# Eight of 22 pairs by Strassen's rule in the down projections of a two-layer encoder

## The chip, the cores and the metric

The kernel runs on one core of one Trainium2 chip. Its time is the device time of that core in microseconds. Five engines run their own queues side by side and wait for each other by semaphores: PE (TensorE, matmuls), DVE (VectorE), ACT (ScalarE), POOL (GpSimd, not used here but for set-up) and SP (SyncE, which issues the loads).

## The reference

A trunk of two layers over 256 tokens of width 2048, in float32. Each layer has a token mixer and a channel mixer, and each of the four does x = x + RMSNorm(f(RMSNorm(x))). What is changed lies in the channel mixer:

```python
D_MODEL, SEQ, D_FF, CONV_WIDTH = 2048, 256, 5632, 3

def conv_glu(h, w_up, conv_w, conv_b, w_down):
    u = h @ w_up
    gate, val = u[..., :D_FF], u[..., D_FF:]
    gate = depthwise_conv3(gate, conv_w, conv_b)
    return (jax.nn.gelu(gate, approximate=False) * val) @ w_down

for i in range(DEPTH):
    ...
    h = rms_norm(x, p['ffn_pre'])
    x = x + rms_norm(conv_glu(h, *p['ffn']), p['ffn_post'])
```

The down projection is the last product: (256 x 5632) by (5632 x 2048).

## The kernel before

**Numbers.** A float32 matrix is held as two parts for the matmuls, a rounded one and the rest: `whi` and `wlo` for weights, `gh` and `gl` for the activations of the channel mixer. A product is three matmuls (L1101, L1102, L1104): hi by hi, lo by hi, hi by lo. The weights arrive whole. `_split` (L159) makes the parts: ACT casts to `whi` (L173) and DVE subtracts it from the raw weights into `wlo` (L174). There are three buffers each for `whi` and `wlo`, and four for the raw weights, all used in turn.

**Chunks.** All weights are cut into chunks of 128 x 1024 floats (512 KB) in one list for the whole program. `weights` (L187) is called once for each chunk: it emits the splits of the chunks up to two further on and the loads (L148) up to five further on. A raw load waits only until its buffer has been split, so SP runs ahead of the other engines.

**Up projection.** `ffn` (L968) works through 11 groups of 512 channels. In each, `proj_t` makes gate and value, the convolution, Gelu and product follow on DVE and ACT, and four tiles of `gh` and `gl` come out. Work that is to lie between the matmuls is written as generators: `now` takes one on, and `tick` runs each up to its next `yield`, once for each chunk.

**Down projection.** `down` (L1002) makes 1024 columns of the output at a time (a half, h = 0 and 1), as two column groups of 512. The 5632 rows are 22 pairs of 256. A plain pair needs two chunks, one for each column group, with 2 token blocks x 2 row blocks x 3 matmuls each: 24 matmuls of 512 columns. `PAIRS` (6) of the pairs go by Strassen's rule in Winograd's form instead. There a pair is a 2 x 2 block product (token blocks, row blocks, column groups), and seven block products do for eight: 21 matmuls. For that, sums of weights (`Seven.sums`, four subtractions on DVE, L76) and sums of tokens (`sums` in `down`, L1010) are needed; the products are added up at the end (`added`, L1045). A seven pair has four steps:

- step 0: the products with the two weight blocks as they are; behind its split the sums of weights are made
- step 1: two products with sums of weights (in place of the blocks of step 0)
- step 2: two products with the second load, its first block by now a sum
- step 3: one product with `seven_t`, 512 columns

The two loads of a pair go to tiles `seven_a` and `seven_b`, one buffer each. The sums of tokens for two pairs at a time (one tile of `gh` and `gl`) take one add of 1024, four of 256, a cast and a subtraction; all three of them run at the start of the down projection.

**Order.** `down_order` (L38) mixes the steps with plain ones: `LEAD` plain steps ahead, then for each pair 0, plain, plain, 1, plain, 2, 3, plain, then the rest of the plain steps. A scheduler under the language sets the final order on each engine, within the dependencies.

Of the kernel before, what the change touches and what calls it, by code (L numbers as in the profile page):

```python
# [30 lines left out]

PAIRS = 6
LEAD = 5, 1


def down_order(h):  # L38

    plain = [("plain", p, o) for o in range(2) for p in range(PAIRS, KF // 2)]  # L40
    out, plain = plain[:LEAD[h]], deque(plain[LEAD[h]:])
    for p in range(PAIRS):
        for j in (0, None, None, 1, None, 2, 3, None):
            out.append(plain.popleft() if j is None else ("seven", p, j))
    return out + list(plain)


class Seven:
# [3 lines left out]


    def __init__(self, a, b):
        self.srcs, self.raw = (a, b), None

    def load(self, model):
        if self.raw is None:
            self.raw = []
            for src, tag in zip(self.srcs, "ab"):  # L60
                raw = model.room.tile([P, 1024], F32, tag=f"seven_{tag}", name=f"seven_{tag}", bufs=1)
                model.nc.sync.dma_start(out=raw, in_=src)
                self.raw.append(raw)

    def step(self, model, j):

        a, b = self.raw
        return (a, a, b, self.t2)[j] if j else a

    def sums(self, model):  # L70
        nc = model.nc
        a, b = self.raw
        self.t2 = model.room.tile([P, 512], F32, tag="seven_t", name="seven_t", bufs=1)
        a0, a1, b0, b1 = a[:, :512], a[:, 512:], b[:, :512], b[:, 512:]
        for out, x, y in ((a0, b0, a0), (self.t2, b1, a0), (a1, a1, self.t2), (b0, b1, b0)):
            nc.vector.tensor_tensor(out=out, in0=x, in1=y, op=ALU.subtract)  # L76

# [9 lines left out]
class Model:  # L87
# [60 lines left out]
    def _load(self, i):  # L148
        if i >= len(self.chunks) or i in self.loaded or i < self.at or i in self.made:
            return  # L150
        if isinstance(self.chunks[i], tuple):
            self.chunks[i][0].load(self)
            self.loaded[i] = None
            return
        raw = self.wp.tile([P, 1024], F32, tag="raw", name="raw", bufs=4)
        self.nc.sync.dma_start(out=raw, in_=self.chunks[i])
        self.loaded[i] = raw
# [810 lines left out]
    def ffn(self, layer, pre):  # L968
        nc, tc = self.nc, self.tc
        with tc.tile_pool(name=f"ffn{layer}", bufs=1) as sp:  # L970
            self.room = sp
            xs = self.xhl
            x = lambda k: xs[k // 4][:, k % 4].rearrange("p a t -> p (a t)")
            gh = [sp.tile([P, 4, T], F32R, name=f"gh{i}") for i in range(NFG)]
            gl = [sp.tile([P, 4, T], F32R, name=f"gl{i}") for i in range(NFG)]
            cw = lambda j, c: self.gain(f"l{layer}_conv_w", j * KF + c)
            norm = self.now(self.pre_norm(sp))
            for gi in range(NFG):
                pg = self.proj_t(KD, x, "acc")
                self.finish(norm)  # L980
                act = []
                for i in range(4):
                    c = 4 * gi + i
                    g = self.joined(sp, sp.tile([P, T], F32, tag="g", name="g", bufs=2), pg[i])
                    y = sp.tile([P, T], F32, tag="yf", name="yf", bufs=4)
                    nc.vector.tensor_tensor(out=g, in0=g, in1=self.rb, op=ALU.mult)
                    nc.scalar.activation(y, g, AF.Identity, scale=cw(1, c), bias=self.gain(f"l{layer}_conv_b", c))
                    nc.vector.scalar_tensor_tensor(out=y[:, 1:], in0=g[:, :T - 1], scalar=cw(0, c), in1=y[:, 1:],
                                                   op0=ALU.mult, op1=ALU.add)
                    nc.vector.scalar_tensor_tensor(out=y[:, :T - 1], in0=g[:, 1:], scalar=cw(2, c),  # L990
                                                   in1=y[:, :T - 1], op0=ALU.mult, op1=ALU.add)
                    nc.scalar.activation(y, y, AF.Gelu)
                    act.append(y)
                pv = self.proj_t(KD, x, "at")
                for i in range(4):
                    u = self.joined(sp, sp.tile([P, T], F32, tag="u", name="u", bufs=2), pv[i])
                    nc.vector.tensor_tensor(out=u, in0=u, in1=self.rb, op=ALU.mult)
                    nc.vector.tensor_tensor(out=u, in0=u, in1=act[i], op=ALU.mult)
                    self.parted(gh[gi][:, i, :], gl[gi][:, i, :], u)
            self.down(gh, gl, 2 * layer + 1, pre)  # L1000

    def down(self, gh, gl, post, pre):  # L1002

        nc = self.nc
        add = lambda out, a, b, op=ALU.add: nc.vector.tensor_tensor(out=out, in0=a, in1=b, op=op)  # L1005
        mm = nc.tensor.matmul
        ss = self.small.tile([P, 2, 4], F32, tag="ss", name="ss", bufs=2)
        seven, m, gains = [], [], []

        def sums():  # L1010

            for i in range(PAIRS // 2):
                tmp = self.act.tile([P, 2, 1024], F32, tag="xm3", name="sums")
                add(tmp[:, 0], gh[i].rearrange("p k t -> p (k t)").bitcast(F32),
                    gl[i].rearrange("p k t -> p (k t)").bitcast(F32))
                a = tmp[:, 0].rearrange("p (q k t f) -> p q k t f", q=2, k=2, t=2)
                s = tmp[:, 1].rearrange("p (q n f) -> p q n f", q=2, n=4)
                a11, a12, a21, a22 = (a[:, :, k, t] for t in range(2) for k in range(2))
                add(s[:, :, 0], a21, a22)
                add(s[:, :, 1], s[:, :, 0], a11, ALU.subtract)  # L1020
                add(s[:, :, 2], a11, a21, ALU.subtract)
                add(s[:, :, 3], a12, s[:, :, 1], ALU.subtract)
                yield
                seven.append(self.act.tile([P, 2, 4, 2, P], F32R, tag=f"xm{i}", name=f"seven{i}"))
                self.parted(seven[i][:, :, :, 0, :], seven[i][:, :, :, 1, :], s)
                yield

        def tokens(k, t):
            return tuple(g[k // 4][:, k % 4, t * P:(t + 1) * P] for g in (gh, gl))

        def summed(p, n):
            return tuple(seven[p // 2][:, p % 2, n, i, :] for i in range(2))

        def operands(kind, p, j, t):

            if kind == "plain":
                return [(2 * j + t, lambda k=2 * p + i: tokens(k, t), i) for i in range(2)]
            if t:
# [117 lines left out]
    def all_chunks(self):  # L1156
# [26 lines left out]
def _tiled(w, n=512):  # L1183

    k, m = w.shape
    b = 1024 // n
    w = w.reshape(k // (b * P), b, P, m // n, n).transpose(3, 0, 2, 1, 4)
    return np.ascontiguousarray(w).reshape(m // n, k // (b * P), P, 1024)


def _rope(pos, dim):

    inv = np.float32(10000.0) ** (-np.arange(0, dim, 2, dtype=np.float32) / np.float32(dim))
    ang = pos.astype(np.float32)[:, None] * inv.astype(np.float32)[None, :]
    c, s = np.cos(ang).astype(np.float32), np.sin(ang).astype(np.float32)
    return np.stack([np.concatenate([c, c], axis=1), np.concatenate([-s, s], axis=1)], axis=1)
# [50 lines left out]
```

## Time and profile before

| | |
|---|---|
| median of three runs | 2062.05 us (2062.04 to 2070.98) |
| span of the profiled execution, first to last instruction | 2060.1 us |
| PE busy in the span | 2043.4 us |
| DVE busy in the span | 1478.4 us |
| ACT busy in the span | 1129.3 us |
| loads and stores | 384 MB, 186 GB/s over the span |
| up projection, layer 0 | about 331 to 823 us |
| down projection, layer 0 | about 823 to 1051 us |
| down projection, layer 1 | about 1818 to 2047 us |

How to read the rows: a row of the timeline has start, duration, engine, line, operation, output<-input, shape and, in brackets, how long the engine had been idle and who released it. A row of a stretch has its bounds and length, then the busy time of PE, its weight loads, DVE, ACT and POOL with the instructions started, PE's granted clock, DMA's busy share and GB/s. A row of loads has the tile, the count, the size and the microseconds from issue to landing. SP's rows show when a load is issued, not how long it takes. Matmuls are pipelined: a row shows 0.39 us, but the next one starts 0.23 us later.

### The profile page before, as it was taken

How to read it: one execution, taken by the hardware profiler on the slowest of the kernel's cores; microseconds unless marked ns; L12 is line 12 of the kernel's file. 1: busy time of each engine (PE TensorE's matmuls, PEld its weight loads, DVE VectorE, ACT ScalarE, POOL GpSimd, SP SyncE). 2: the span in 40 equal slices, each digit the busy share in tenths (PEclk: the TensorE clock that was granted, in tenths of full speed). 3: DMA queues.
4: the chain of work that ended last, by engine and by line, in shares of the span. 5: the costliest groups of instructions: out<-in, count | busy, mean ns of one | idle time of the engine just before them, and what ended most of it. 6: DMA issues, size and time to landing. Idle time of an engine off the chain costs nothing.

```text
span 2060.1 us, 29196 instructions
## 1 busy us (share of the span) xinstructions
PE 2043.4 (99%) x10905; PEld 1750.0 (85%) x10905; DVE 1478.4 (72%) x2263; ACT 1129.3 (55%) x1753; POOL 0.2 (0%) x4
## 2 busy tenths in 40 slices
PE   9999999999999999999999999999999999999998
PEld 7888888888888888888878998888888888888886
DVE  6877757766766767878787875676766766787877
ACT  6655546555555555555465664555555555554553
POOL 0000000000000000000000000000000000000000
PEclk9999999999999999999999999999999999999999
DMA  8545566666566666566655445566566566556664
GB/s 318 176 153 161 166 197 193 186 194 193 185 194 191 185 194 189 184 211 197 203 179 170 124 134 173 176 210 189 185 193 193 184 195 193 185 184 205 204 206 141
DMA packets 108717, 385.96 MB, mean 187 GB/s; under 512 B 12064, under 2 KB 12576, under 8 KB 108576
## 3 DMA queue, kind: packets, MB, share of 16 engines
q1 hardware_dynamic: 108288, 383.83, 59.3%
q8 instruction: 85, 1.39, 0.3%
q14 instruction: 56, 0.46, 0.1%
q10 hardware_dynamic: 288, 0.28, 0.0%
HBM read 381.96 MB, written 2.10 MB: 186 GB/s over the span
## 4 chain that ended last, share of the span: by engine, by line
PE 96%; DVE 3%; issue 0%; ACT 0%; DMA 0%; DVEq 0%; SPq 0%; ACTq 0%
PE ps L244 31%; PE ps L245 16%; PE ps L230 8%; PE ps L231 8%; PE ps L232 8%; PE ps L1104 7%; PE ps L1101 7%; PE ps L1102 7%; PE ps L537 1%; PE ps L300 1%; DVE x L454 1%; DVE wlo L174 1%; PE ps L478 0%; DVE sums L1005 0%; DMA raw<-in_w_in 0%
## 5 line engine op out<-in xcount | busy, mean ns | idle before, releaser
L174 DVE TENSOR_TENSOR wlo<-raw,whi 128x1024 fp32r<-128x1024 f32 (+1 forms) x662 | 807.6, 1221 | 490.3 <-ACT whi L173 487.6
L173 ACT CAST whi<-raw 128x1024 fp32r<-128x1024 f32 (+1 forms) x662 | 694.3, 1050 | 642.7 <-PE ps L244 302.4
L244 PE MATMUL ps<-xhl,whi 128*128 128x512 f32 x2816 | 978.7, 394 | 1.0 <-DVE xhl L591 1.0
L245 PE MATMUL ps<-xhl,wlo 128*128 128x256 f32 x2816 | 779.2, 277 | 0.0
L244 PEld LDWEIGHTS ps<-xhl,whi 128*128 128x128 f32 x2816 | 527.6, 188 | 123.1 <-DVE xhl L591 2.0
L245 PEld LDWEIGHTS ps<-xhl,wlo 128*128 128x128 f32 x2816 | 528.9, 188 | 1.0 <-DVE wlo L174 0.5
L1101 PE MATMUL ps<-whi,gh 128*128 128x512 f32 x584 | 227.3, 389 | 0.0
L1102 PE MATMUL ps<-whi,gl 128*128 128x512 f32 x584 | 227.2, 389 | 0.0
L1104 PE MATMUL ps<-wlo,gh 128*128 128x512 f32 x584 | 182.0, 390 | 0.8 <-DVE wlo L174 0.8
L230 PE MATMUL ps<-whi,xhl 128*128 128x512 f32 x352 | 138.7, 395 | 0.9 <-ACT whi L173 0.8
L231 PE MATMUL ps<-wlo,xhl 128*128 128x512 f32 x352 | 137.6, 391 | 0.0
L232 PE MATMUL ps<-whi,xhl 128*128 128x512 f32 x352 | 137.2, 390 | 0.0
L1104 PEld LDWEIGHTS ps<-wlo,gh 128*128 128x128 f32 x584 | 109.1, 188 | 25.2 <-DVE wlo L174 2.7
L1101 PEld LDWEIGHTS ps<-whi,gh 128*128 128x128 f32 x584 | 109.6, 188 | 22.8
L1102 PEld LDWEIGHTS ps<-whi,gl 128*128 128x128 f32 x584 | 109.6, 188 | 22.8
L230 PE MATMUL ps<-whi,oh 128*128 128x512 f32 x256 | 100.0, 390 | 0.0
L231 PE MATMUL ps<-wlo,oh 128*128 128x512 f32 x256 | 99.7, 389 | 0.0
L232 PE MATMUL ps<-whi,ol 128*128 128x512 f32 x256 | 99.6, 389 | 0.0
L305 ACT COPY half<-ps 128x256 f32<-128x256 f32 x176 | 65.1, 370 | 43.9 <-PE ps L244 34.6
L230 PEld LDWEIGHTS ps<-whi,xhl 128*128 128x128 f32 x352 | 66.0, 188 | 14.5 <-ACT whi L173 1.1
L232 PEld LDWEIGHTS ps<-whi,xhl 128*128 128x128 f32 x352 | 66.1, 188 | 13.9
L231 PEld LDWEIGHTS ps<-wlo,xhl 128*128 128x128 f32 x352 | 66.3, 188 | 13.4 <-DVE wlo L174 0.9
(211 smaller groups left out, 2061.0 us busy)
## 6 DMA issues: line engine op xcount, KB each, us to landing
raw<-in_w_up SPq DMA_DIRECT2D x352, 512.0 KB, 4.1
raw<-in_w_down SPq DMA_DIRECT2D x128, 512.0 KB, 3.9
raw<-in_w_in SPq DMA_DIRECT2D x88, 512.0 KB, 3.7
raw<-in_w_out SPq DMA_DIRECT2D x64, 512.0 KB, 4.1
seven_a<-in_w_down SPq DMA_DIRECT2D x24, 512.0 KB, 4.5
seven_b<-in_w_down SPq DMA_DIRECT2D x24, 512.0 KB, 4.2
gb<-in_post SPq DMA_DIRECT2D x16, 256.0 KB, 3.8
raw<-in_w_qn SPq DMA_DIRECT2D x8, 512.0 KB, 3.6
```

The costliest lines, as they stand in the source:

```text
L173: self.nc.scalar.copy(hi[:, s], raw[:, s])
L174: self.nc.vector.tensor_tensor(out=lo[:, s], in0=raw[:, s], in1=hi[:, s].bitcast(F32), op=ALU.subtract)
L230: mm(ps, lh, rh, start=start, stop=False)
L231: mm(ps, lh, rl, start=False, stop=False)
L232: mm(ps, ll, rh, start=False, stop=stop)
L244: mm(out[i], hi[:, s], x(k), start=k == 0, stop=False)
L245: mm(out[i][:, :T], lo[:, s], x(k)[:, :T], start=False, stop=k == nk - 1)
L300: self.tc.keep_in_program_order(self.nc.tensor.transpose(out, x, self.ident))
L305: self.nc.scalar.copy(b, ps[:, T:])
L1101: mm(bank, xh, w[0][:, c], start=start, stop=False)
L1102: mm(bank, xl, w[0][:, c], start=False, stop=False)
L1104: mm(bank, xh, w[1][:, c], start=False, stop=stop)
```

## The change

Eight pairs in place of six go by the rule. The order of steps gets closer: seven steps for a pair (0, plain, 1, plain, 2, 3, plain) or six (without the last plain one). In the first half, pairs 0 to 3 have seven and 4 to 7 have six; in the second the even ones have seven, the odd ones six. The lead of the first half is 4 plain steps instead of 5. The token sums of the first two tiles, half of the four that are now needed, are made in the up projection behind groups 0 and 1. The two weight tiles become one of 2048 columns, with each half loaded when it is free, and the host turns the blocks of one chunk so that two of the sums are one subtraction of 1024. Space for the larger tiles comes from a smaller scratch area for DMA.

```diff
-PAIRS = 6
-LEAD = 5, 1
+PAIRS = 8
+EARLY = 2
+LEAD = 4, 1
...
     for p in range(PAIRS):
-        for j in (0, None, None, 1, None, 2, 3, None):
+        room = p < PAIRS // 2 if h == 0 else p % 2 == 0
+        for j in (0, None, 1, None, 2, 3, None) if room else (0, None, 1, None, 2, 3):
             out.append(plain.popleft() if j is None else ("seven", p, j))
...
     def load(self, model):
-        if self.raw is None:
-            self.raw = []
-            for src, tag in zip(self.srcs, "ab"):
-                raw = model.room.tile([P, 1024], F32, tag=f"seven_{tag}", name=f"seven_{tag}", bufs=1)
-                model.nc.sync.dma_start(out=raw, in_=src)
-                self.raw.append(raw)
+        self.raw = model.sevens()
+        for n in range(2):
+            if self.srcs[n] is not None and model.seven_free[n]:
+                model.nc.sync.dma_start(out=self.raw[:, 1024 * n:1024 * n + 1024], in_=self.srcs[n])
+                self.srcs[n], model.seven_free[n] = None, False
+        return self.srcs == [None, None]

     def step(self, model, j):
-        a, b = self.raw
-        return (a, a, b, self.t2)[j] if j else a
+        if 0 < j < 3:
+            model.seven_free[j - 1] = True
+        return self.t2 if j == 3 else self.raw[:, 1024:] if j == 2 else self.raw[:, :1024]

     def sums(self, model):
...
-        for out, x, y in ((a0, b0, a0), (self.t2, b1, a0), (a1, a1, self.t2), (b0, b1, b0)):
-            nc.vector.tensor_tensor(out=out, in0=x, in1=y, op=ALU.subtract)
+        b21, b11, b22 = x[:, :512], x[:, 512:1024], x[:, 1536:]
+        sub = lambda out, a, b: nc.vector.tensor_tensor(out=out, in0=a, in1=b, op=ALU.subtract)
+        sub(x[:, 512:1536], x[:, 1024:], x[:, 512:1536])
+        sub(self.t2, b22, b11)
+        sub(b21, b21, self.t2)
...
                     self.parted(gh[gi][:, i, :], gl[gi][:, i, :], u)
-            self.down(gh, gl, 2 * layer + 1, pre)
+                if gi < EARLY:
+                    seven = seven if gi else []
+                    self.now(self.token_sums(gh, gl, gi, seven))
+            self.down(gh, gl, 2 * layer + 1, pre, seven)
...
+    def sevens(self):
+
+        if self.seven_raw is None:
+            self.seven_raw = self.room.tile([P, 2048], F32, tag="seven", name="seven_raw", bufs=1)
+            self.seven_free = [True, True]
+        return self.seven_raw
...
+            for i in range(EARLY, PAIRS // 2):
+                yield from self.token_sums(gh, gl, i, seven)
...
+def _turned(w):
+
+    w[::2, :PAIRS] = np.roll(w[::2, :PAIRS], 512, axis=-1)
+    return w
...
-    nc = bacc.Bacc("TRN2", target_bir_lowering=False, num_devices=1)
+    nc = bacc.Bacc("TRN2", target_bir_lowering=False, num_devices=1,
+                   dynamic_dma_scratch_size=1024)
```

`token_sums` holds the same operations on `gh` and `gl` as the body of `sums` did before, with a `yield` after each of four parts.

What this makes of DVE's queue, in the first half of layer 0's down projection. First before, from the split of step 0 of a pair to that of step 1 (`raw` is a plain chunk; the numbers tell buffers apart):

```order
L174 TENSOR_TENSOR wlo_8451<-seven_a_8410,whi_8450 128x1024
L174 TENSOR_TENSOR wlo_8463<-raw_8424,whi_8462 128x1024
L76 TENSOR_TENSOR seven_a_8410<-seven_b_8412,seven_a_8410 128x512
L76 TENSOR_TENSOR seven_t_8454<-seven_b_8412,seven_a_8410 128x512
L76 TENSOR_TENSOR seven_b_8412<-seven_b_8412 128x512
L76 TENSOR_TENSOR seven_a_8410<-seven_a_8410,seven_t_8454 128x512
L174 TENSOR_TENSOR wlo_8481<-raw_8442,whi_8480 128x1024
L174 TENSOR_TENSOR wlo_8491<-seven_a_8410,whi_8490 128x1024
```

The same engine after the change, from step 1 of pair 6 to step 1 of pair 7, the last two of the first half:

```order
L179 TENSOR_TENSOR wlo_8660<-seven_raw_7959,whi_8659 128x1024
L179 TENSOR_TENSOR wlo_8670<-raw_8644,whi_8669 128x1024
L179 TENSOR_TENSOR wlo_8687<-seven_raw_7959,whi_8686 128x1024
L179 TENSOR_TENSOR wlo_8700<-seven_t_8640,whi_8699 128x512
L179 TENSOR_TENSOR wlo_8716<-seven_raw_7959,whi_8715 128x1024
L179 TENSOR_TENSOR wlo_8732<-raw_8691,whi_8731 128x1024
L78 TENSOR_TENSOR seven_raw_7959<-seven_raw_7959 128x1024
L78 TENSOR_TENSOR seven_t_8719<-seven_raw_7959 128x512
L78 TENSOR_TENSOR seven_raw_7959<-seven_raw_7959,seven_t_8719 128x512
L179 TENSOR_TENSOR wlo_8739<-seven_raw_7959,whi_8738 128x1024
```

The first four rows are steps 1, plain, 2 and 3 of pair 6. Step 0 of pair 7 follows step 3 at once, and between its split and that of step 1 stand one plain split and three sums, where there were two plain splits and four sums.

PE's queue before, from the last matmuls of the plain step ahead of step 1 to the first of the plain step behind it:

```order
L1102 MATMUL ps_7999<-whi_8480,gl4_3124 128x512
L1104 MATMUL ps_7999<-wlo_8481,gh4_3113 128x512 x2
L1101 MATMUL ps_8120<-whi_8490,seven1_8092 128x512
L1102 MATMUL ps_8120<-whi_8490,seven1_8092 128x512
L1101 MATMUL ps_7997<-whi_8490,gh1_3110 128x512
L1102 MATMUL ps_7997<-whi_8490,gl1_3121 128x512
L1104 MATMUL ps_8120<-wlo_8491,seven1_8092 128x512
L1104 MATMUL ps_7997<-wlo_8491,gh1_3110 128x512
L1101 MATMUL ps_7998<-whi_8506,gh4_3113 128x512
```

And after, at step 1 of pair 6:

```order
L1130 MATMUL ps_8018<-whi_8652,gl7_3127 128x512
L1132 MATMUL ps_8018<-wlo_8653,gh7_3116 128x512 x2
L1129 MATMUL ps_8101<-whi_8659,seven3_8168 128x512
L1130 MATMUL ps_8101<-whi_8659,seven3_8168 128x512
L1129 MATMUL ps_8016<-whi_8659,gh3_3112 128x512
L1130 MATMUL ps_8016<-whi_8659,gl3_3123 128x512
L1129 MATMUL ps_8017<-whi_8669,gh7_3116 128x512
L1130 MATMUL ps_8017<-whi_8669,gl7_3127 128x512
L1132 MATMUL ps_8101<-wlo_8660,seven3_8168 128x512
L1132 MATMUL ps_8016<-wlo_8660,gh3_3112 128x512
```

Two matmuls with `whi` of the plain step behind now stand ahead of the two with `wlo` of step 1. It is so in pairs 0, 5, 6 and 7 of the first half (three in pair 0) and in pairs 2, 4 and 6 of the second, but in no other pair.

SP's queue in the same stretch, before (`seven_a` and `seven_b` of one pair, then the next pair's first):

```order
L62 DMA seven_a_8410<-in_w_down0 128x1024
L156 DMA raw_8466<-in_w_down0 128x1024
L62 DMA seven_b_8412<-in_w_down0 128x1024
L156 DMA raw_8510<-in_w_down0 128x1024
L156 DMA raw_8542<-in_w_down0 128x1024
L156 DMA raw_8560<-in_w_down0 128x1024
L62 DMA seven_a_8528<-in_w_down0 128x1024
```

And after, where one load of `seven_raw` is the first half of a pair's weights and the next the second half:

```order
L64 DMA seven_raw_7959<-in_w_down0 128x1024
L161 DMA raw_8723<-in_w_down0 128x1024
L64 DMA seven_raw_7959<-in_w_down0 128x1024
L161 DMA raw_8752<-in_w_down0 128x1024
L64 DMA seven_raw_7959<-in_w_down0 128x1024
L161 DMA raw_8770<-in_w_down0 128x1024
```

Between the two halves of one pair's weights still lies one plain load, but between pairs there is now one where there were three.

More of the change, by code (lines that the diff above doesn't have):

```diff
@@ L54, in __init__ @@
     def __init__(self, a, b):
-        self.srcs, self.raw = (a, b), None
+        self.srcs, self.raw = [a, b], None
     def load(self, model):
-        if self.raw is None:
-            self.raw = []
-            for src, tag in zip(self.srcs, "ab"):
-                raw = model.room.tile([P, 1024], F32, tag=f"seven_{tag}", name=f"seven_{tag}", bufs=1)
-                model.nc.sync.dma_start(out=raw, in_=src)
-                self.raw.append(raw)
+        self.raw = model.sevens()
[4 more added lines that the diff above has]
+        return self.srcs == [None, None]
     def step(self, model, j):
-        a, b = self.raw
-        return (a, a, b, self.t2)[j] if j else a
+        if 0 < j < 3:
+            model.seven_free[j - 1] = True
+        return self.t2 if j == 3 else self.raw[:, 1024:] if j == 2 else self.raw[:, :1024]
     def sums(self, model):
-        nc = model.nc
-        a, b = self.raw
+        nc, x = model.nc, self.raw
         self.t2 = model.room.tile([P, 512], F32, tag="seven_t", name="seven_t", bufs=1)
-        a0, a1, b0, b1 = a[:, :512], a[:, 512:], b[:, :512], b[:, 512:]
-        for out, x, y in ((a0, b0, a0), (self.t2, b1, a0), (a1, a1, self.t2), (b0, b1, b0)):
-            nc.vector.tensor_tensor(out=out, in0=x, in1=y, op=ALU.subtract)
+        b21, b11, b22 = x[:, :512], x[:, 512:1024], x[:, 1536:]
[3 more added lines that the diff above has]
+        sub(b21, b21, self.t2)
 G_NAMES = ["l0_mix_pre", "l0_ffn_pre", "l1_mix_pre", "l1_ffn_pre",
@@ L151, in _load @@
         if isinstance(self.chunks[i], tuple):
-            self.chunks[i][0].load(self)
-            self.loaded[i] = None
+            if self.chunks[i][0].load(self):
+                self.loaded[i] = None
             return
@@ L973, in ffn @@
             x = lambda k: xs[k // 4][:, k % 4].rearrange("p a t -> p (a t)")
+            self.seven_raw = None
             gh = [sp.tile([P, 4, T], F32R, name=f"gh{i}") for i in range(NFG)]
@@ L999, in ffn, with token_sums, down @@
                     self.parted(gh[gi][:, i, :], gl[gi][:, i, :], u)
-            self.down(gh, gl, 2 * layer + 1, pre)
-    def down(self, gh, gl, post, pre):
+                if gi < EARLY:
[7 more added lines that the diff above has]
+        return self.seven_raw
+    def token_sums(self, gh, gl, i, seven):
+        nc = self.nc
+        add = lambda out, a, b, op=ALU.add: nc.vector.tensor_tensor(out=out, in0=a, in1=b, op=op)
+        if i < EARLY:
+            tmp = self.room.tile([P, 2, 1024], F32, tag="seven", name="sums", bufs=1)
+        else:
+            tmp = self.act.tile([P, 2, 1024], F32, tag="xm3", name="sums")
+        add(tmp[:, 0], gh[i].rearrange("p k t -> p (k t)").bitcast(F32),
+            gl[i].rearrange("p k t -> p (k t)").bitcast(F32))
+        yield
+        a = tmp[:, 0].rearrange("p (q k t f) -> p q k t f", q=2, k=2, t=2)
+        s = tmp[:, 1].rearrange("p (q n f) -> p q n f", q=2, n=4)
+        a11, a12, a21, a22 = (a[:, :, k, t] for t in range(2) for k in range(2))
+        add(s[:, :, 0], a21, a22)
+        add(s[:, :, 1], s[:, :, 0], a11, ALU.subtract)
+        yield
+        add(s[:, :, 2], a11, a21, ALU.subtract)
+        add(s[:, :, 3], a12, s[:, :, 1], ALU.subtract)
+        yield
+        home, tag = (self.room, f"early{i}") if i < EARLY else (self.act, f"xm{i - EARLY}")
+        seven.append(home.tile([P, 2, 4, 2, P], F32R, tag=tag, name=f"seven{i}", bufs=1))
+        self.parted(seven[i][:, :, :, 0, :], seven[i][:, :, :, 1, :], s)
+        yield
+    def down(self, gh, gl, post, pre, seven):
         nc = self.nc
@@ L1007, in down @@
         ss = self.small.tile([P, 2, 4], F32, tag="ss", name="ss", bufs=2)
-        seven, m, gains = [], [], []
+        m, gains = [], []
         def sums():
[L1012 to L1026, printed above, removed]
+            for i in range(EARLY, PAIRS // 2):
+                yield from self.token_sums(gh, gl, i, seven)
         def tokens(k, t):
@@ L1039, in operands @@
                 return []
-            return [[(4, lambda: tokens(2 * p, 0), 0), (0, lambda: tokens(2 * p + 1, 0), 1)],
-                    [(5, lambda: summed(p, 0), 0), (1, lambda: tokens(2 * p + 1, 1), 1)],
+            return [[(4, lambda: tokens(2 * p, 0), 1), (0, lambda: tokens(2 * p + 1, 0), 0)],
+                    [(5, lambda: summed(p, 0), 1), (1, lambda: tokens(2 * p + 1, 1), 0)],
                     [(7, lambda: summed(p, 2), 0), (2, lambda: summed(p, 3), 1)],
@@ L1227 @@
         arr[f"w_up{l}"] = _tiled(inp[f"l{l}_w_up"])
-        arr[f"w_down{l}"] = _tiled(inp[f"l{l}_w_down"])
+        arr[f"w_down{l}"] = _turned(_tiled(inp[f"l{l}_w_down"]))
     arr["w_in1"] = _tiled(inp["l1_w_in"][:, :1024])
```

## The prediction

> **What bounds the kernel now.** I read the page's busy times and its chain first, then the busy times by stretch, PE's waits in a down projection, and DVE, ACT and PE there in order of time.
>
> ```profile
> span 2060.1 us, 29196 instructions
> PE 2043.4 (99%) x10905; PEld 1750.0 (85%) x10905; DVE 1478.4 (72%) x2263; ACT 1129.3 (55%) x1753; POOL 0.2 (0%) x4
> PE 96%; DVE 3%; issue 0%; ACT 0%; DMA 0%; DVEq 0%; SPq 0%; ACTq 0%
> ...
> 976.00:991.65 15.65, 15.65 (x70) 12.95 (x69) 11.51 (x13) 7.91 (x9) 0.00 (x0) 1.00 0.61 203
> ...
> PE ps L1104 <- DVE wlo L174: 0.4, 1, 0.4
> ```
>
> PE sets the time: 99% busy, 96% of the chain, clock 1.00. The fourth row is one pair of the down projection in layer 0 with the plain steps woven into it: 21 + 48 = 69 matmuls in 15.65 us, with DVE busy for 11.51 of them. A matmul of 512 columns costs PE 0.2268 us. The last row is all that PE waits for DVE in a whole down projection (815 to 1065 us; layer 1 has the same). So PE has nothing to win but its own matmuls, and everything to lose if a factor comes late.
>
> **What the change removes.** A plain pair costs 24 matmuls in a half of the outputs, a seven pair 21. Two more pairs, two halves, two layers, three matmuls each: 24 x 0.2268 = **5.4 us less** on PE.
>
> **What it moves.** I call the steps of a pair A (block product 0), C, E, F (products 1 to 3) and B, D, G the plain steps between. Before, the order was A B B C D E F G; now it is A B C D E F G in long pairs and A B C D E F in short ones. Between A and C stand the sums of weights, which C needs. DVE's and ACT's rows for one pair of before:
>
> ```profile
> 876.17 1.23 DVE L174 TENSOR_TENSOR wlo<-seven_b,whi 128x1024 fp32r<-128x1024 f32 x1 [1.45 <-ACT whi L173]
> ...
> 881.62 1.22 DVE L174 TENSOR_TENSOR wlo<-seven_a,whi 128x1024 fp32r<-128x1024 f32 x1
> 882.76 1.22 DVE L174 TENSOR_TENSOR wlo<-raw,whi 128x1024 fp32r<-128x1024 f32 x1
> 883.89 0.68 DVE L76 TENSOR_TENSOR seven_a<-seven_b,seven_a 128x512 f32<-128x512 f32 x1
> 884.61 0.69 DVE L76 TENSOR_TENSOR seven_t<-seven_b,seven_a 128x512 f32<-128x512 f32 x1
> 885.22 0.69 DVE L76 TENSOR_TENSOR seven_b<-seven_b 128x512 f32<-128x512 f32 x1
> 885.82 0.69 DVE L76 TENSOR_TENSOR seven_a<-seven_a,seven_t 128x512 f32<-128x512 f32 x1
> ...
> 887.71 1.23 DVE L174 TENSOR_TENSOR wlo<-seven_a,whi 128x1024 fp32r<-128x1024 f32 x1
> ...
> 880.53 1.06 ACT L173 CAST whi<-seven_a 128x1024 fp32r<-128x1024 f32 x1 [0.31 <-PE ps L1102]
> ...
> 886.62 1.05 ACT L173 CAST whi<-seven_a 128x1024 fp32r<-128x1024 f32 x1 [1.63 <-DVE seven_a L76]
> ...
> 880.10 0.39 PE L1102 MATMUL ps<-whi,seven 128*128 128x512 f32 x1
> ...
> 884.18 0.39 PE L1101 MATMUL ps<-whi,gh 128*128 128x512 f32 x1
> ```
>
> There are three buffers for whi, so A's cast (880.53) starts when PE ends the last whi matmul of the step three before A (880.10 + 0.39, and 0.04 for the signal). From there the chain runs A's split on DVE (881.62), B's split (882.76), the sums (883.89), C's cast (886.62), C ready for PE (887.71): 7.18 us. PE starts A at 884.18 and C 30 matmuls later, at 890.98. Before, C's factors were 3.3 us early.
>
> **The chain after.** The sum of 1024 elements isn't in the trace as such; a subtraction of that size is:
>
> ```profile
> 832.31 1.22 DVE L1005 TENSOR_TENSOR sums<-gh,gl 128x1024 f32<-128x1024 f32 x1
> ```
>
> The three sums now each need the one before: 1.22 + 0.04 + 0.69 + 0.04 + 0.69 + 0.11 to the cast = 2.79, against 2.73 from 883.89 to 886.62. DVE has a little less work per pair; the chain is no shorter.
> [...]
>
> How far is PE from C when A's cast starts?
> - Long pair behind a long one: the step three before A is E; 2 lo matmuls of E, then F, G, A, B: 35 matmuls less 0.20 (the tail of the last one, and the signal) = 7.73 us. The chain takes 7.18 + 0.06 = 7.24. C is 0.49 early, no wait.
> - Any pair behind a short one: it is D; 2 of D, then E, F, A, B: 29 matmuls less 0.20 = 6.37 us. Here B's cast also waits for E, 1.36 behind A's cast and not 0.96, which adds 0.22 to the chain: 7.46. **C is 1.09 us late**, and PE has nothing else in its queue.
>
> That is six pairs in a layer: 5, 6, 7 of the first half (4 to 7 are short) and 2, 4, 6 of the second (odd ones are short). Their order on PE, with two matmuls of D put between C's, covers the wlo of C but not its whi.
>
> **The transfer.** The second half of the weights may be loaded once E of the pair before is split, and the 1024-wide sum needs it. What SP does is seen here, with three answers of the trace on time to landing for 860.35, 861.49 and 862.62, one for 847.72, and the range over all:
>
> ```profile
> 860.35 0.33 SPq L62 DMA_DIRECT2D seven_a<-in_w_down  x1
> 861.49 0.33 SPq L156 DMA_DIRECT2D raw<-in_w_down  x1
> 862.62 0.33 SPq L62 DMA_DIRECT2D seven_b<-in_w_down  x1
> ...
> 877.43 0.33 SPq L62 DMA_DIRECT2D seven_b<-in_w_down  x1
> ...
> seven_a<-in_w_down SPq DMA_DIRECT2D x1, 512.0 KB, 3.6
> raw<-in_w_down SPq DMA_DIRECT2D x1, 512.0 KB, 4.6
> seven_b<-in_w_down SPq DMA_DIRECT2D x1, 512.0 KB, 4.8
> ...
> seven_b<-in_w_down SPq DMA_DIRECT2D x1, 512.0 KB, 6.5
> ...
> DMA to landing us min/median/max: 3.1/4.2/6.5
> ```
>
> The load goes out as the split ends (876.17 + 1.23, then 877.43). After a short pair's C, D and E are split back to back, 1.14 apart, so three loads go out 1.14 apart, as at 860.35: the third landed 4.8 us later. I take 4.8; the ends are 4.2 and 6.5.
> Count from PE's start of C. Where C was on time, its cast started 1.58 before (0.49 + 1.09), C's split at -0.49, D's +0.65, E's 1.79, done 3.02; load 3.05, landed 7.85, sum 7.90; C of the next pair is ready 2.79 + 1.09 later, at 11.78; due after 45 matmuls, 10.20: **1.58 late**. Where C itself waited, its split starts at 0 and E's at 2.28, and the same sum gives 12.27: **2.07 late**. The second holds for pairs 6 and 7 of the first half, the first for the other four. Per layer 4 x 1.58 + 2 x 2.07 = 10.5; **20.9 us** in all. With 4.2 to landing the places cost 1.09 (chain) and 1.47, 14.6 in all; with 6.5, 3.28 and 3.77, 41.3.
> [...]
>
> **The rest.**
>
> ```profile
> 834.58 1.09 DVE L1005 TENSOR_TENSOR sums<-sums 128x256 f32<-128x256 f32 x3
> ...
> 840.73 1.20 PE L1104 MATMUL ps<-wlo,gh 128*128 128x512 f32 x4 [0.37 <-DVE wlo L174]
> ...
> 340.00:820.00 480.00, 480.00 (x2776) 419.69 (x2775) 331.91 (x527) 263.33 (x399) 0.00 (x0) 1.00 0.63 192
> ...
> 930.00:945.00 15.00, 15.00 (x68) 12.34 (x67) 14.57 (x20) 8.71 (x13) 0.00 (x0) 1.00 0.57 183
> ```
>
> - Into the down projection PE waited 0.37 for DVE. Half of the token sums are gone from there, but C of pair 0 comes 12 matmuls earlier behind A. It comes out even. At the start of the second half DVE is full (14.57 of 15.00), and D there comes some 0.4 late. I put 1 us on all this (from -0.8, both waits gone, to +3).
> - The token sums moved up cost DVE 1.22 + 4 x 0.36 + 1.22 = 3.9 us each (the sum of gh and gl, four of the kind in the first row here, the split). The up projection leaves DVE 148 of 480 us, some 13 in each of its 11 groups. Nothing on PE; if uncovered, at most 4 x 3.9 = 16 us.
> - New order of the 512-column blocks and less scratch memory: nothing, in one the host does the work, the other touches no queue of the page.
>
> Sum: -5.4 + 20.9 + 1.0 = +16.5. The profiled execution spans 2060.1 and the median of three runs is 2062.05, 1.95 more, which I keep: **2078.5 us**.
>
> **Rivals.**
> 1. *No late C: faster.* If C's factors come at least 1.09 us (or the load 1.6 to 2.1) earlier than worked out, only the matmuls are left, and the two small waits: 2062.05 - 5.4 - 0.7 = 2055.9. For it: ACT and DVE are idle a third of a pair's time (11.51 and 7.91 of 15.65). Against: they idle because no buffer is free, and the change adds none.
> 2. *The chain alone is late.* Loads land in under 4.4: 12 x 1.09 = 13.1, so -5.4 + 13.1 + 1.0 = +8.7, 2070.8.
> 3. *Loads as slow as at 847.72* (6.5): -5.4 + 41.3 + 1.0, 2099.
> 4. *The change doesn't do what it says*: excluded, the new program has 24 matmuls fewer.
>
> **How the numbers follow.** Forecast 0.58 (2072 to 2087, loads of 4.2 to 5.4 us), rival 2 0.20, rival 1 0.13, rival 3 0.09. The forecast and rival 2 hold 0.78; with an error of 0.5 us per late place (12 x 0.5 = 6 below 2070.8) the range goes from 2064 to 2087. A measurement here tells some 0.5% (10.3 us) from no change; that bound is 2072.4, between rival 2 and the forecast. Slower: the forecast but for its lower edge (0.53), rival 3 (0.09) and a little of rival 2: 0.65. Same: 0.32. Faster by over 0.5% needs more than the matmuls can give: 0.03.
>
> **What would show it.** Right: PE waits in each down projection, six of 1 to 2 us, on ACT's whi in a step of products behind a short pair, none behind long ones; DVE idle before the 1024-wide sum, ended by a DMA; a down projection some 8 us longer. If the wait is there but DVE isn't held by a DMA, rival 2. If PE has no such wait, my chain is wrong, at the step from A's cast to PE's distance. PE waits in the first groups of an up projection would mean that the moved token sums aren't covered.

## The result, and the profile after

| | before | after |
|---|---|---|
| median of five runs | 2062.05 us | 2086.6 us (2082.94 to 2097.09) |
| ratio, with its 95% interval | | 1.0115 (1.0087 to 1.0142) |
| span of the profiled execution | 2060.1 us | 2091.9 us (in an execution of 2094.01) |
| down projection, layer 0 / 1, from the start of its first matmul row to the start of its last | 231.94 / 231.93 us | 241.74 / 244.77 us |

The change makes the kernel 1.2% slower, and the interval of the ratio lies wholly above 1. The page of after, its busy times and the chain:

```profile
span 2091.9 us, 29228 instructions
...
PE 2054.9 (98%) x10881; PEld 1747.9 (84%) x10881; DVE 1518.4 (73%) x2291; ACT 1133.9 (54%) x1771; POOL 0.2 (0%) x4
...
PE 86%; DVE 7%; DMA 3%; ACT 2%; issue 2%; DVEq 0%; ACTq 0%; SPq 0%
```

The 24 matmuls are gone (10905 before), yet the chain, 96% on PE before, now has 12% on DVE, DMA and ACT (3% before, all on DVE). PE's waits in the two down projections (830 to 1080 and 1840 to 2092 us), then the long ones of layer 0 in order of time:

```profile
PE ps L1129 <- ACT whi L178: 9.8, 8, 1.7
...
PE ps L1129 <- ACT whi L178: 10.9, 8, 2.7
...
902.55 0.50 PE L1129 MATMUL ps<-whi,seven 128*128 128x512 f32 x1 [1.69 <-ACT whi L178]
914.76 0.50 PE L1129 MATMUL ps<-whi,seven 128*128 128x512 f32 x1 [1.38 <-ACT whi L178]
926.93 0.50 PE L1129 MATMUL ps<-whi,seven 128*128 128x512 f32 x1 [1.59 <-ACT whi L178]
...
976.88 0.50 PE L1129 MATMUL ps<-whi,seven 128*128 128x512 f32 x1 [1.56 <-ACT whi L178]
...
1001.74 0.50 PE L1129 MATMUL ps<-whi,seven 128*128 128x512 f32 x1 [1.38 <-ACT whi L178]
1026.98 0.50 PE L1129 MATMUL ps<-whi,seven 128*128 128x512 f32 x1 [1.59 <-ACT whi L178]
```

Six waits of 1.4 to 1.7 us: the C of pairs 5, 6, 7 in the first half and of 2, 4, 6 in the second, each behind a short pair. No C behind a long pair waits over 0.4 us in this layer. In layer 1 the same six wait 1.35 to 2.70 us, and one A behind a short pair 0.60.

The total needs one caution: in this execution the up projection of layer 1 goes at 115 matmuls per 20 us, at a granted clock of 1.00, where that of layer 0 and both of before have 117 or 118, and from the last matmul row of one down projection to the first of the next it is 772.22 us in place of 763.37; executions of the kernel before lie as far apart (2070.98 and 2062.05, the longer one without a profile), so that I take these 9 us for no effect of the change and compare the down projections from first to last matmul, beside the medians. The rows are of the up projections of this execution, layer 0 and layer 1 (length, then PE busy and its matmuls):

```profile
480.00:500.00 20.00, 20.00 (x118) 17.48 (x117) 14.22 (x23) 12.34 (x20) 0.00 (x0) 1.00 0.61 185
1500.00:1520.00 20.00, 20.00 (x115) 17.33 (x115) 13.28 (x21) 10.77 (x17) 0.00 (x0) 1.00 0.61 188
```

The downs grew by 9.8 and 12.8 us, by rows like these:

```profile
822.75 0.39 PE L1101 MATMUL ps<-whi,gh 128*128 128x512 f32 x1
...
1054.69 0.61 PE L1104 MATMUL ps<-wlo,gh 128*128 128x512 f32 x2
```

```profile
823.07 0.39 PE L1129 MATMUL ps<-whi,gh 128*128 128x512 f32 x1
...
1064.81 0.61 PE L1132 MATMUL ps<-wlo,gh 128*128 128x512 f32 x2
```

The first pair of rows is of before, the second of after, layer 0; the numbers of the table come from such rows, start to start.

What holds C? The chain of waits of after between two of the late C's (start, duration, what):

```profile
902.53 1.24 DVE wlo L179
...
903.78 3.65 DMA seven_raw<-in_w_down
...
907.53 1.06 ACT whi L178
...
909.75 1.03 DVE wlo L179
...
910.89 1.23 DVE seven_raw L78
...
912.14 0.70 DVE seven_t L78
...
912.87 0.70 DVE seven_raw L78
```

and ACT's casts in the same place, and what ACT and DVE wait for loads of this tile in the down projection of layer 0 (820 to 1070 us):

```profile
901.45 1.04 ACT L178 CAST whi<-seven_raw 128x1024 fp32r<-128x1024 f32 x1 [4.58 <-DVE seven_raw L78]
...
907.53 1.05 ACT L178 CAST whi<-seven_raw 128x1024 fp32r<-128x1024 f32 x1 [2.61 <-DMA seven_raw<-in_w_down]
...
913.67 1.04 ACT L178 CAST whi<-seven_raw 128x1024 fp32r<-128x1024 f32 x1 [4.13 <-DVE seven_raw L78]
```

```profile
ACT whi L178 <- DMA seven_raw<-in_w_down: 15.3, 6, 2.7
...
DVE seven_raw L78 <- DMA seven_raw<-in_w_down: 0.7, 3, 0.4
```

It is a loop. C's split ends, the first half of the weight tile is free and its load goes out (903.78), A's cast waits for it (907.53), the sums follow, and they release the next C's cast at 913.67. The cast before that was at 901.45: 12.2 us a turn. PE gives a short pair 45 matmuls, 10.2 us; a long one 57, 12.9. The prediction had a load in this place too, but that of the second half, which holds the 1024-wide sum. But here DVE waits for a load only 0.7 us in all, and ACT 15.3 (in layer 1 it is 1.6 and 16.8). So my first reading of the result (theory T) put the first half's load in the place of the second's.

### The profile page after: what moved, and what is told of

Its sections match the earlier page's. It is cut to its first block, busy times and chain, and to the rows that moved or that the text cites. A ratio compares the mean times of both kernels' runs of the same rounds, so it can differ in the third digit from the quotient of the medians.

```text
span 2091.9 us, 29228 instructions
## 1 busy us (share of the span) xinstructions
PE 2054.9 (98%) x10881; PEld 1747.9 (84%) x10881; DVE 1518.4 (73%) x2291; ACT 1133.9 (54%) x1771; POOL 0.2 (0%) x4
## 4 chain that ended last, share of the span: by engine, by line
PE 86%; DVE 7%; DMA 3%; ACT 2%; issue 2%; DVEq 0%; ACTq 0%; SPq 0%
PE ps L249 31%; PE ps L250 16%; PE ps L235 8%; PE ps L236 8%; PE ps L237 8%; PE ps L1129 4%; PE ps L1130 4%; PE ps L1132 4%; DMA seven_raw<-in_w_down 2%; DVE wlo L179 2%; DVE seven_raw L78 2%; ACT whi L178 2%; PE ps L542 1%; PE ps L305 1%; DVE seven_t L78 1%
## 5 line engine op out<-in xcount | busy, mean ns | idle before, releaser
L179 DVE TENSOR_TENSOR wlo<-raw,whi 128x1024 fp32r<-128x1024 f32 (+1 forms) x646 | 788.0, 1221 | 451.5 <-ACT whi L178 448.6
L178 ACT CAST whi<-raw 128x1024 fp32r<-128x1024 f32 (+1 forms) x646 | 676.7, 1049 | 586.0 <-PE ps L249 323.7
L1129 PE MATMUL ps<-whi,gh 128*128 128x512 f32 x544 | 213.1, 392 | 0.6 <-ACT whi L178 0.6
L1130 PE MATMUL ps<-whi,gl 128*128 128x512 f32 x544 | 212.7, 391 | 0.0
L178 ACT CAST whi<-seven_raw 128x1024 fp32r<-128x1024 f32 x96 | 100.7, 1049 | 164.6 <-DVE seven_raw L78 119.5
L1132 PE MATMUL ps<-wlo,gh 128*128 128x512 f32 x544 | 170.9, 391 | 0.1
L179 DVE TENSOR_TENSOR wlo<-seven_raw,whi 128x1024 fp32r<-128x1024 f32 x96 | 117.4, 1223 | 61.8 <-ACT whi L178 56.1
L1132 PEld LDWEIGHTS ps<-wlo,gh 128*128 128x128 f32 x544 | 101.6, 188 | 22.7 <-DVE wlo L179 2.2
L235 PEld LDWEIGHTS ps<-whi,xhl 128*128 128x128 f32 x352 | 66.0, 188 | 14.6 <-ACT whi L178 1.3
```

The source lines that it names most:

```text
L178: self.nc.scalar.copy(hi[:, s], raw[:, s])
L179: self.nc.vector.tensor_tensor(out=lo[:, s], in0=raw[:, s], in1=hi[:, s].bitcast(F32), op=ALU.subtract)
L235: mm(ps, lh, rh, start=start, stop=False)
L1129: mm(bank, xh, w[0][:, c], start=start, stop=False)
L1130: mm(bank, xl, w[0][:, c], start=False, stop=False)
L1132: mm(bank, xh, w[1][:, c], start=False, stop=stop)
```

## The experiments

The times in the table are medians; the ratio is to the kernel before on the same chip, over all executions of both and not of the medians, with its 95% interval.

| run | what | median us | ratio | down, layer 0 / 1 |
|---|---|---|---|---|
| e3_two_tiles | two weight tiles | 2069.18 | 1.0038 (1.0018 to 1.0058) | 235.36 / 235.37 |
| e4_bufs4 | four buffers of whi, wlo | 2088.12 | 1.0108 (1.0077 to 1.0139) | 241.51 / 241.92 |
| e5_early1 | control of the last | 2096.74 | 1.0140 (1.0110 to 1.0170) | 243.21 / 245.60 |
| e_long | long pairs, lead 3 | 2072.42 | 1.0056 (1.0033 to 1.0079) | 235.01 / 234.48 |
| e8_first_two | first half twice | 2088.73 | 1.0113 (1.0089 to 1.0138) | 244.24 / 240.92 |
| e9_second_two | second half twice | 2077.46 | 1.0072 (1.0047 to 1.0096) | 239.11 / 240.07 |
| e7b_one_abb | A B B C, one tile | 2110.76 | 1.0214 (1.0187 to 1.0240) | 253.72 / 251.70 |
| e6b_two_abb | A B B C, two tiles | 2058.18 | 0.9988 (0.9970 to 1.0006) | 229.83 / 229.86 |
| e_short | all pairs short | 2119.58 | 1.0268 (1.0232 to 1.0304) | 260.13 / 260.62 |
| e10_four_sums | four sums of 512 | 2084.61 | 1.0093 (1.0066 to 1.0120) | 242.27 / 241.59 |
| e11_long_lead1 | long pairs, lead 1 | 2069.27 | 1.0021 (1.0004 to 1.0039) | 233.75 / 234.00 |
| e12_long_lead2 | long pairs, lead 2 | 2070.65 | 1.0040 (1.0024 to 1.0057) | 234.24 / 233.17 |

### Is it the tile, the split's buffers, or something else?

```diff
...
-        if self.seven_raw is None:
-            self.seven_raw = self.room.tile([P, 2048], F32, tag="seven", name="seven_raw", bufs=1)
-            self.seven_free = [True, True]
-        return self.seven_raw
+        self.seven_turn ^= 1
+        n = self.seven_turn
+        if self.seven_raw[n] is None:
+            home, tag = (self.act, "xm2") if n else (self.room, "seven")
+            self.seven_raw[n] = home.tile([P, 2048], F32, tag=tag, name=f"seven_raw{n}", bufs=1), [True, True]
+        return self.seven_raw[n]
```

> The changed kernel, with two weight tiles in turn for the seven pairs (the second in space that the activations leave free), so that a pair's loads wait for nothing that the pair just before holds. Theory T (the loop through the one tile makes C late: C's split frees the first half, its load holds A's cast, then the sums, then C's cast): the loads land early, what is left is the chain from A's cast behind three buffers, 1.09 us in 12 places, so 2060.1 to 2062.05 - 5.4 + 13 + 1 = about 2070 to 2072, and no row of ACT or DVE is ended by a load of this tile. Rival R (buffers of the split alone; the loads were hidden anyway): as the changed kernel, 2083 to 2087. Rival S (the late C is not the reason, but the token sums or the order are): also 2083 to 2087, with the PE waits behind short pairs smaller.

```diff
-EARLY = 2
+EARLY = 1
...
-        hi = self.wp.tile([P, 1024], F32R, tag="whi", name="whi", bufs=3)
-        lo = self.wp.tile([P, 1024], F32R, tag="wlo", name="wlo", bufs=3)
+        hi = self.wp.tile([P, 1024], F32R, tag="whi", name="whi", bufs=4)
+        lo = self.wp.tile([P, 1024], F32R, tag="wlo", name="wlo", bufs=4)
```

> The changed kernel with four buffers each for the split's two parts instead of three; for space, the token sums of one tile instead of two are made in the up projection. Theory T: A's cast still waits for the load of the first half, so C stays late by most of its 2 us a place; 2076 to 2085. Rival R (three buffers hold A's cast): the waits of PE for ACT's cast vanish, 2056 to 2060.

The control has only the first line of that edit:

> The changed kernel with the token sums of one tile instead of two made in the up projection; the control for the run with four buffers. All theories of the late C: as the changed kernel, 2083 to 2087 (at most 1 us more at the start of the down projection). Rival S (token sums in the up projection cost what was lost): 2072 to 2080, half of the loss gone.

Two tiles bring 2069.18, 17 us less than after, with 235.4 us in both downs. PE's rows at three of the six places there:

```profile
910.44 0.50 PE L1132 MATMUL ps<-whi,seven 128*128 128x512 f32 x1 [0.60 <-ACT whi L179]
921.68 0.50 PE L1132 MATMUL ps<-whi,seven 128*128 128x512 f32 x1 [0.59 <-ACT whi L179]
932.93 0.50 PE L1132 MATMUL ps<-whi,seven 128*128 128x512 f32 x1 [0.57 <-ACT whi L179]
```

The waits are even now, 0.6 us where they had been 1.4 to 1.7. No row of ACT or DVE is ended by a load of this tile any more; the loads are out, and what holds A's cast is a buffer that PE has not yet left. A's cast and C's, ahead of the second of these waits:

```profile
914.44 1.05 ACT L179 CAST whi<-seven_raw 128x1024 fp32r<-128x1024 f32 x1 [1.64 <-PE ps L1133]
...
920.58 1.05 ACT L179 CAST whi<-seven_raw 128x1024 fp32r<-128x1024 f32 x1 [3.73 <-DVE seven_raw L79]
```

From C to C it is 921.68 - 910.44 = 11.24 us here, where 45 matmuls take 10.21: a late C costs 1.03 us, more than the 0.6 of its row. A row counts the wait from the modelled end of the matmul before, 0.39 us behind its start, when the next one would have started after 0.23; and the first matmul behind the wait holds the next for 0.33 in place of 0.23. Around the twelve late C's of this run PE loses 0.34 to 0.38 us more than the rows say.

Four buffers leave the downs at 241.5 and 241.9, 1.7 and 3.7 us below their control; the median, 2088.12, lies above both ranges that I gave for it. So the transfers through the one tile are the larger part, the buffers of the split the smaller. The control is no better than after (its downs are 0.8 to 1.5 us longer; that this comes from the token sums left for them is likely, but wasn't tried), so the moved token sums aren't what was lost. Its median is 10 us higher, of which its downs explain 2.3.

### Which half of the tile?

Here the halves are tiles of their own, and one of them gets two buffers (index 0 in the first run, 1 in the second). The wide sum can't reach over two tiles and becomes two of 512.

```diff
-        sub(x[:, 512:1536], x[:, 1024:], x[:, 512:1536])
+        sub(b11, b12, b11)
         sub(self.t2, b22, b11)
         sub(b21, b21, self.t2)
+        sub(b12, b22, b12)
...
+                raw = self.act.tile([P, 1024], F32, tag="xm2", name="seven_more", bufs=1)
+                self.seven_raw.append((raw, [True]))
+            now[0] = self.seven_raw[2]
```

> The changed kernel with two buffers in turn for the first half of the weights of a seven pair, one for the second; the 1024-wide sum of weights becomes two of 512, as before the change. Theory T (the load of the first half, which waits for C's split of the pair before and holds A's cast): the loop is gone, what is left is some 6.2 us a layer as with two whole tiles; down projections of about 235.5 us from first to last matmul, 2068 to 2071 where the up projection is fast. Rival P (the prediction's step: the load of the second half, which waits for E's split and holds the 1024-wide sum): as the changed kernel, down projections of 241 to 245 us, 2082 to 2087.

> The mirror of the run before: two buffers in turn for the second half of the weights, one for the first. Theory T: as the changed kernel, 2080 to 2087, down projections of 240 to 245 us, A's cast held by loads. Rival P: 2068 to 2071, down projections of about 235.5 us.

Theory T falls, and so does rival P as it stood: with two buffers for the first half the time stays (2088.73), as P has it, but with two for the second it drops to 2077.46, about half of what two whole tiles bring, and not to P's 2068 to 2071. DVE, ACT and SP of e8_first_two:

```profile
900.89 1.04 ACT L181 CAST whi<-seven_more 128x1024 fp32r<-128x1024 f32 x1 [4.23 <-DVE seven_more L80]
...
904.25 1.22 DVE L182 TENSOR_TENSOR wlo<-seven_raw,whi 128x1024 fp32r<-128x1024 f32 x1
...
905.49 0.33 SPq L66 DMA_DIRECT2D seven_raw<-in_w_down  x1
906.01 1.05 ACT L181 CAST whi<-seven_raw 128x1024 fp32r<-128x1024 f32 x1 [1.66 <-PE ps L1140]
...
910.57 0.69 DVE L80 TENSOR_TENSOR seven_raw<-seven_raw 128x512 f32<-128x512 f32 x1 [0.88 <-DMA seven_raw<-in_w_down]
...
913.30 1.04 ACT L181 CAST whi<-seven_raw 128x1024 fp32r<-128x1024 f32 x1 [4.87 <-DVE seven_raw L80]
```

A's cast (906.01) no longer waits for a load, but for PE's buffer. The first sum (910.57) now waits for the second half: E's split ends at 905.47, its load goes out 0.02 later, the sum starts 5.1 after that, and C's cast follows 2.73 later. From C's cast to C's cast that is 12.4 us, as long as the turn through the first half. This is the loop of the prediction, step by step. And where the second half is doubled, the other stays:

```profile
900.55 1.05 ACT L181 CAST whi<-seven_raw 128x1024 fp32r<-128x1024 f32 x1 [4.09 <-DVE seven_raw L80]
...
906.55 1.05 ACT L181 CAST whi<-seven_raw 128x1024 fp32r<-128x1024 f32 x1 [2.54 <-DMA seven_raw<-in_w_down]
...
912.64 1.04 ACT L181 CAST whi<-seven_raw 128x1024 fp32r<-128x1024 f32 x1 [4.08 <-DVE seven_raw L80]
```

12.1 us a turn. Two loops lie side by side in the change, within 0.3 us of each other. A profile names only the last releaser, and with A's cast late by the first half, the second half's load is already there when the sum gets its turn: in after the load of 906.06 takes 4.7 us and lands 0.1 ahead of the sum (910.89). That is why after shows 15.3 us of ACT waiting for this tile and only 0.7 of DVE in layer 0, though the second half holds at least as hard. In layer 1 there is a place where it shows. There the second half's load goes out at 2032.33 and takes 6.1 us, the sum waits for it, and PE's wait at that C, 2.70 us, is the longest of all:

```profile
2038.53 1.23 DVE L78 TENSOR_TENSOR seven_raw<-seven_raw 128x1024 f32<-128x1024 f32 x1 [1.38 <-DMA seven_raw<-in_w_down]
```

### Out of the loops

The next two runs put both plain steps between A and C; the second also has the two tiles.

```diff
-        for j in (0, None, 1, None, 2, 3, None) if room else (0, None, 1, None, 2, 3):
+        for j in (0, None, None, 1, None, 2, 3) if room else (0, None, None, 1, 2, 3):
```

> The order of the run before with the one weight tile of the change. Theory T: the loop from C's cast through the load to the next C's cast takes some 12.2 us and a pair behind a short one gives 10.2, wherever A stands in it, so PE now waits at A or C for most of 2 us in 12 places; down projections of 238 to 242 us, 2075 to 2083. Rival R (only the distance from A to C counts): no wait, 2056 to 2060.

> Two whole weight tiles in turn, and in each pair both plain steps that stand ahead of E are put between A and C (A B B C D E F and A B B C E F instead of A B C D E F G and A B C D E F). From A's cast to C there are 41 matmuls at the least instead of 29, so that the chain of 7.46 us has 9.1 us. Theory T and the 1.09 of the chain: no late C at all, down projections of 229 to 231 us, 2056 to 2060, faster than before. Rival S (other parts of the change cost some 6 us a layer): as with two tiles alone, 2069.

With one tile it gets worse: 28 us above the upper edge of what I expected, 24 above after. Its waits are longer, and they cost more than they last. One of them, and a stretch of 1 us behind it (the last column but two is the granted clock):

```profile
900.29 0.50 PE L1129 MATMUL ps<-whi,gh 128*128 128x512 f32 x1 [1.90 <-ACT whi L178]
...
902.00:903.00 1.00, 1.00 (x4) 0.74 (x3) 1.00 (x2) 0.14 (x1) 0.00 (x0) 0.50 0.00 0
```

Behind a pause of 1.90 us PE runs at half its clock; more on this below. In layer 0 ten waits last 13.2 us by PE's rows. With 0.33 more for each, and some 1.6 for each of the five that the half clock follows, that is 24.5, and the down is 23.9 longer than with two tiles. With two tiles no C is late: in 820 to 1060 us PE's list of waits has no row of this projection, and the chain and a short pair (902 to 912.2 us; its 46 are 45 matmuls in 10.20 us and the end of one more) are

```profile
PE 98%; DVE 1%; ACT 0%; issue 0%; DMA 0%; DVEq 0%; SPq 0%; ACTq 0%
...
902.00:912.20 10.20, 10.20 (x46) 8.26 (x46) 8.89 (x9) 5.47 (x7) 0.00 (x0) 1.00 0.69 206
```

The downs take 229.83 and 229.86 us, 2.1 less than before. The 12 matmuls of a layer are worth 2.7, so 0.6 is lost elsewhere in the projection. This version is the best of all: median 2058.18 against 2062.16 of before on the same chip, though the interval of the ratio still takes in 1, so that "faster" is shown for the downs and not for the whole.

### Twice the places, and none

All pairs short (`room = False`): 28 places in place of 12.

> The changed kernel with six steps for every pair (seven places behind a short one in a half, 28 in all, in place of 12). Theory (loops of 12.2 and 12.4 us against the 10.20 us that PE has in a short pair, 2.0 to 2.3 us a place): 28 x 2.0 to 2.3 over 2057.5, 2113 to 2122, more where a pause lowers the granted clock. The prediction's first size, 1.09 by the chain of buffers alone: 2088. Rival S (no place matters): as the changed kernel.

Its downs are 30.3 and 30.8 us above the 229.8 without late C's. With 14 places in a layer that is 2.2 us a place, and the median, 2119.58, lies in the range that the loops gave. Now the sums in the old form (the four subtractions of the diff above, in one tile), and long pairs throughout (`room = p < PAIRS - 1`) with three leads in the first half:

> The changed kernel with the sums of weights by four instructions of 512 columns, as before the change, in place of one of 1024 and two of 512. Theory (the loops make C late, and the chain of sums is as long in both forms, 2.73 against 2.79 us): as the changed kernel, down projections of 241 to 245 us, 2082 to 2087, at most 0.06 us less in a late place. Rival (the wide sum, which needs both halves, is what holds C): 2070 to 2077, since two of four sums need less.

> The changed kernel with seven steps for every pair but the last of a half (the lead in the first half is 3 plain steps for that), so that no pair stands behind a short one. The work is the same. Theories T and R alike: no late C, the waits of PE for ACT's cast vanish but for those at the start of a half; 2056 to 2060. Rival S (something else in the change costs the time: token sums, order of the blocks, the wider sum): 2075 to 2087, nearly as the changed kernel.

> The changed kernel with seven steps for every pair but the last of a half, as in the run with long pairs, but one plain step as lead in both halves, so that four plain steps stay for the end of a half instead of two in the first. Theory L (behind a long pair the loops through the one tile, 12.2 us through the first half and 12.4 through the second, fit into PE's 12.93, and what the earlier run of long pairs lost lies in the one pause of 2.3 us a layer behind the last pair, for the adds of the products, and in the lower granted clock behind it): both are gone, down projections of 229.5 to 231.5 us, 2057 to 2061. Rival (the one tile costs some us even behind long pairs): down projections of 234 us and more, 2067 to 2071.

> The run of long pairs with two plain steps as lead in the first half, between the three (a pause of 2.3 us for the adds behind the last pair) and the one (a pause of 2.0 us for DVE's token sums ahead of pair 1) of the runs before. Theory L (behind long pairs the one tile costs nothing, each single pause and the clock behind it cost some 4 us a layer): with neither pause, down projections of 229.5 to 231 us, 2057 to 2061; with one of the two pauses left, 233 to 235 us, 2065 to 2070. Rival (the one tile costs behind long pairs too): 2065 to 2070 without a pause of over 1 us.

The form of the sums makes no difference that can be measured: 242.27 and 241.59, beside 241.74 and 244.77. So the two sums of 512 in e8_first_two and e9_second_two aren't what those runs show.

None of the three runs with long pairs reaches the 2056 to 2061 that I gave for them without a pause. The loops don't hold there: between 860 us and the last pair of layer 0, PE has no wait for whi in e_long and e11_long_lead1, and one of 0.9 us in e12_long_lead2. What takes their place stands at the ends. In e_long, beside waits of 0.76 and 0.33 us at the first pairs, it is one long wait in each layer, where the second half starts and the adds of the products still hold their banks:

```profile
942.63 0.50 PE L1129 MATMUL ps<-whi,gh 128*128 128x512 f32 x1 [2.28 <-DVE m L1046]
```

In e11_long_lead1 it is DVE, full with token sums and splits at the second pair:

```profile
844.81 1.37 PE L1132 MATMUL ps<-wlo,gh 128*128 128x512 f32 x4 [2.03 <-DVE wlo L179]
```

With lead 2 there are waits of 0.54 and 1.51 us at the first pairs. Also, from the start of the last matmul row of the program's last down projection to the end of the span it is 12.0 to 13.0 us in these three, 10.1 in before and in after. So theory L holds for the pairs in the middle, but not its sum: I found no lead that avoids every pause. That the longer end comes from fewer plain steps behind the last pair is my reading; it wasn't tried by itself.

## Why the prediction was right, point by point

- **Range and side.** 2086.6 lies in 2064 to 2087, 8 us above the 2078.5 forecast and 0.4 below the edge; two of the five executions lie above it. That it lies inside is in part luck. The edge isn't what its own sum gives, either: loads of 5.4 us are 12 x 0.6 = 7.2 above the forecast, 2085.7. Slower was the likelier side.
- **The matmuls, -5.4.** Right: 24 fewer on PE. e6b_two_abb gets 4.2 of it in the downs.
- **The places.** Right in count and position: six in a layer, all at C behind a short pair, released by ACT's cast.
- **The chain behind three buffers, 1.09 a place.** Shown by e3_two_tiles, where of the late C's only it is left: 1.03 from C to C, and over a layer 235.36 - 229.83 = 5.5 us in six places, 0.92 each. That the buffers hold it is read from A's casts there, which PE releases; two tiles with four buffers weren't tried.
- **The transfer, 1.58 or 2.07 a place.** The step is real (e8_first_two, 12.4 us a turn), but it is one of two. The prediction took the first half's load as early enough, and that step failed: this load, out when C's split ends, takes 3.65 us, and holds A's cast by 2.6 us at 907.53. It changed what the trace shows more than the time, because the two loops run side by side. The sign that I gave for the transfer, DVE held by a DMA ahead of the 1024-wide sum, is weak: 0.7 us in layer 0, and 1.6 in layer 1, most of it at one place (2038.53). By my own rule that would have been rival 2, which e3_two_tiles excludes: with the loads out of the way the time falls by 17 us, so they aren't hidden.
- **The size.** From C to C in two short pairs it is 914.76 - 902.55 = 12.21 us, less 10.21 for 45 matmuls: 2.0 late, forecast 2.07. Against before less its matmuls (2 x 229.2) the downs lose 241.74 + 244.77 - 458.4 = 28.1 us, forecast 20.9 + 1.0. Counted from PE's rows around each wait, at 0.2268 us a matmul, the twelve places are 23.2 of it (20.9 forecast, so this term was 2.3 too small), four waits of 0.31 to 0.60 elsewhere 3.3 (forecast 1.0, under the rest), and the half clock behind the pause of 2.70 us is 1.6, which the sum had not at all. The other 1.9 us by which the median moved were not located.
- **Rest, +1.0.** e6b_two_abb loses 0.6 a layer without any late C, 1.2 in all. PE has no wait in the up projection of layer 0, so the token sums there are hidden, as predicted.
- **Rival 2.** It had the loads land in under 4.4 us. In after they take 3.65 to 6.1 at the places shown, with a median of 4.6 over this tile's 64, and in e8_first_two the one of 905.49 takes 5.0, where I had 4.8.

## What to carry to other kernels

A buffer that is loaded anew for each group of steps closes a loop (freed, loaded, prepared, used, freed); its turn has to be shorter than the shortest group on the bound engine, 12.2 us against 10.2 here. Write down every such loop, not only the one that the wait names: two of nearly equal length hide each other, and a cure of one alone brought nothing for the first half, and half of the gain for the second. The cure was one more tile and two plain steps between A and C; the tile alone left 7 us, the steps alone made it worse.

## What the hardware showed that was not expected

A pause of PE can cost more than its length, beyond the 0.33 us above. After, layer 1, in stretches of 1 us behind the pause of 2.70 us that ends at 2042.41:

```profile
2042.00:2043.00 1.00, 0.58 (x2) 0.48 (x3) 0.60 (x1) 1.00 (x2) 0.00 (x0) 0.98 0.00 0
2043.00:2044.00 1.00, 1.00 (x4) 0.80 (x3) 1.00 (x2) 1.00 (x2) 0.00 (x0) 0.50 0.00 0
...
2045.00:2046.00 1.00, 1.00 (x4) 0.71 (x4) 1.00 (x2) 0.00 (x0) 0.00 (x0) 0.50 0.71 266
2046.00:2047.00 1.00, 1.00 (x5) 0.83 (x4) 0.57 (x1) 0.00 (x0) 0.00 (x0) 0.81 0.69 258
2047.00:2048.00 1.00, 1.00 (x6) 0.81 (x5) 0.00 (x0) 0.01 (x1) 0.00 (x0) 1.00 0.85 344
```

The granted clock is 0.50 for 0.04 + 3 + 0.38 = 3.4 us (the first and the last from 0.98 and 0.81 as a mean of 1.00 and 0.50). From 2043.01 to 2046.41 PE's rows have 8 matmuls, 0.43 us apart in place of 0.23, which costs 1.6 us.

The length of the pause doesn't decide it alone. The shortest pause in the runs' down projections that the half clock followed is 1.76 us, and the longest that it didn't follow is 2.90, with a granted clock of 1.00 in each of the six stretches of 1 us behind it:

```profile
850.82 0.50 PE L1129 MATMUL ps<-whi,seven 128*128 128x512 f32 x1 [1.76 <-ACT whi L178]
...
853.00:854.00 1.00, 1.00 (x3) 0.76 (x3) 1.00 (x2) 0.19 (x1) 0.00 (x0) 0.50 1.00 197
...
2046.86 0.50 PE L1129 MATMUL ps<-whi,seven 128*128 128x512 f32 x1 [2.90 <-ACT whi L178]
...
2049.00:2050.00 1.00, 1.00 (x6) 0.81 (x6) 1.00 (x2) 0.22 (x1) 0.00 (x0) 1.00 0.86 197
```

The first two rows are of e_short, the others of e5_early1. What else decides is open: 1.76 us was enough once, and 2.90 once was not. The half clock, once there, lasted 3.4 us by the same sum at three more places: behind the pause of 1.90 us at 900.29 in e7b_one_abb, of 1.95 at 977.24 in e8_first_two and of 2.03 at 844.81 in e11_long_lead1.
